# Sixty product slabs in each feed-forward part, eight short last tiles

## The chip, the cores and the metric

The kernel runs on one core of one Trainium2 chip. Times are device microseconds of one execution. A row of the trace names an engine: PE does matrix products (PEld its weight loads), DVE elementwise work, ACT scalar functions and copies, POOL a few DMAs, and SP issues most of the weight transfers. A matrix product sums into a bank, 128 partitions by 512 fp32 columns of the accumulator memory; DVE and ACT read banks from there.

## What is computed

A decoder trunk of two layers on 256 tokens of width 2048, in fp32. What the change touches is the feed-forward step at the end of both layers, a squared-ReLU map to width 8192 and back:

```python
D_MODEL = 2048
D_FF = 4 * D_MODEL
...
def squared_relu_mlp(h, w1, w2):
    z = jax.nn.relu(h @ w1)
    return (z * z) @ w2
...
for i in range(DEPTH):
    if i == N_A_LAYERS:
        sk1, sk2, sv = shared_kv(x, kv_norm, w_kv, k_norm, cos, sin)
    ...
    x = x + jnp.concatenate([token_out, mem_out], axis=-1) @ w_out[i]
    x = x + squared_relu_mlp(rms_norm(x, ffn_norm[i]), w_ff1[i], w_ff2[i])
return x
```

## The kernel before, in words

**Two halves of a number.** PE's fast fp32 format keeps only part of an fp32 number. Every operand is therefore held as a rounded half `hi` and a remainder `lo`, and a product is hi x hi + lo x hi + hi x lo. Weights arrive as fp32 from DRAM (`Feed.load`), in blocks of 128x128 grouped by four. A quad is prepared by a cast on ACT (L177) and a subtraction on DVE (L178) into the rings `hi_ring` and `lo_ring`, six slots of 512 columns. The feed makes these preparations in one fixed list and runs three of them ahead of the job that PE is at (`AHEAD` in `fill`). Both engines work off their queues in order, so a late split holds whatever stands behind it.

**Ordinary tiles.** `a_part` multiplies a block by the 256 tokens in two matmuls: L430 has `hi` as the fixed operand and streams the tokens' [hi | lo] side by side, 512 columns, and L432 has `lo` and streams 256 columns. The two halves of the bank must then be added on DVE after an eviction by ACT (L758). `c_tile` makes the same product as three matmuls of 256 columns (L444 to L446), all into one half of a bank, so nothing has to be added afterwards.

**A feed-forward part** (`ffn`, called for l = 0 and l = 1) takes the stretches from about 252 to 928 us and from about 1325 us to the end. It computes 64 up tiles of 128 units each (`up_tile`): 16 blocks of `w_ff1`, eviction L758, add L815, ReLU (L819 to L823), square L826 into `stage`, and from there `convert` splits the result into `z` and forms, for every pair of tiles, four sums of quarter blocks (`combine`, L790 to L793; `sums_low`). Later, and partly in between, it multiplies by `w_ff2`.

**Slabs.** Most of the product with `w_ff2` is done by a Strassen-Winograd scheme: two blocks of rows by two times 512 columns are multiplied by seven products instead of eight. Such a piece is a slab (`slab_jobs`): four jobs with 1 or 2 products each, a product being three 512-column matmuls (L861, L863, L864), summed in seven banks. The weights of a slab need sums as well: `first_sum` brings the sum of two transfers by a DMA on SP's queue and an accumulating one on POOL's (L152), and `_prepare` makes two further ones on DVE (L201, L215). There are two column groups: g = 1 holds output tiles 0 to 7, g = 0 tiles 8 to 15, and both use the same seven banks. When the group changes, `swap` copies the seven banks to SBUF (L928) and the other group's back (L920, in `restore`), all on ACT. Rows are grouped in batches of four slabs, h; the order of the groups is 0 1, 1 0, 0 1 and so on, so the group changes once a batch. A slab of index i needs the up tiles 2i and 2i+1 with their sums. There are 56 slabs in a part (`PER_PART`): i = 0 to 23 in both groups, then i = 24 to 31 in group 0 alone. Then five swaps take place and, at the last change, `close_left`, which folds the seven banks of group 1 with DVE and ACT into four quarters. `turn_left` transposes these on PE (L973) and adds them to the residual.

**When the slabs run.** `early` and `late` give the up tile at which each slab is due. `due` issues the jobs that are due, every four blocks of an up tile; it stops when 16 jobs (four slabs) are left. `at(d, ...)` puts a follow-up operation d ticks later; a tick comes with every job and every quad.

**The end of a part** is `last`. What group 1 has not done with slabs, the rows of up tiles 48 to 63, is done as eight down tiles 0 to 7 of 16 blocks each (`down_tile`: `a_part`, eviction, add, multiply by the row scale, add to the residual). In the second part the last one, n = 7, uses `c_tile` and needs no eviction. The 16 left jobs stand between quads of these tiles (`ends`). `finish_banks`, at tile 5, folds group 0's banks, and its four transposed pieces (`ct`, L1012) follow some ticks later. As each output tile is complete, `done(n)` starts the next stage's preparation with it (first part: `x_kv`, L326) or its transfer to the output (second part).

A scheduler orders the program on each engine; `feed.order` adds an order between two instructions without a wait. One such order puts the ReLU of tile 2 behind the last cast issued before it (L821).

Of the kernel before, what the change touches and what calls it, by code (L numbers as in the profile page):

```python
# [18 lines left out]
T = 256  # L19
# [4 lines left out]
NH = 725  # L24
NBLK = 5796
SLOTS, AHEAD, LOADS, RAWS = 6, 3, 3, 4
PER_PART = 56
CN = 0.5 ** (1.0 / 3.0)
LNC = math.log(CN)

# [68 lines left out]
class Feed:  # L99


    def __init__(self, tc, wst, wpool, rows, plan, dry):
        self.tc, self.nc, self.wst, self.wpool, self.rows = tc, tc.nc, wst, wpool, rows
        self.plan, self.dry = plan, dry
        self.pos = 0
        self.slab_no = 0
        self.lp = self.pp = 0
        self.raw = {}
        self.split = {}
        self.t1 = None  # L110
        self.loads_ahead = LOADS
        self.t1_of = [None] * 3
        self.behind = None
        self.gate = None
        if not dry:
            self.hi = wpool.tile([P, SLOTS * 512], F32R, name="hi_ring")
            self.lo = wpool.tile([P, SLOTS * 512], F32R, name="lo_ring")
            self.busy = [False] * SLOTS
            self.at = 0
# [52 lines left out]
    def _split(self, job, src, n):  # L172
        a = self._slots(n)
        if a is None:
            return False
        hi, lo = self.hi[:, a * 512 : (a + n) * 512], self.lo[:, a * 512 : (a + n) * 512]
        self.last_cast = self.nc.scalar.copy(hi, src)  # L177
        low = self.nc.vector.tensor_sub(lo, src, hi.bitcast(F32))  # L178
        if job[0] == "S":
            self.last_low = low  # L180
        if self.behind:
            self.order(low, self.behind)
            self.behind = None
        self.split[job] = (hi, lo, range(a, a + n))
        return True
# [103 lines left out]
def program(ctx, tc, plan, dry, xT, memT, par, lam, cst, wst, yT):  # L289
# [437 lines left out]
    def ffn(l, xs, tags, done):  # L727
# [27 lines left out]
        def evict(ps):  # L755
            x = outs[cnt[0] % 2]
            cnt[0] += 1
            nc.scalar.copy(x, ps)  # L758
            return x

        def when(ready, fn):
            fn() if ready() else at(1, lambda: when(ready, fn))
# [45 lines left out]
        def up_tile(i, ps, between=None):  # L808
            a_part(ps, "w_ff1", l, i, range(NK), xs, between=between)
            if i == 0:  # L810
                r.append(rstd_from("x"))
                at(3, lambda: r.append(columns("x", "o")[1]))
                at(6, lambda: nc.scalar.activation(r[0], r[0], AF.Square))
            y = evict(ps)[:, 0 : 2 * T]
            at(1, lambda: nc.vector.tensor_add(y[:, 0:T], y[:, 0:T], y[:, T : 2 * T]))  # L815
            d = 3 if i == 2 else 2

            def relu():
                one = nc.scalar.activation(y[:, 0:T], y[:, 0:T], AF.Relu)  # L819
                if i == 2 and not dry:  # L820
                    feed.order(one, feed.last_cast.ins.name)  # L821

            at(d, relu)  # L823

            def square():
                nc.scalar.activation(stage[i % 8], y[:, 0:T], AF.Square)  # L826
                at(1, lambda: convert(i))

            at(d, square, 2)

        def down_tile(n, ps, between=None):
            ks = range(3 * NK, 4 * NK)
            if l == 1 and n == 7:
                c_tile(ps, "w_ff2", l, n, ks, z)
                x = outs[cnt[0] % 2]
                nc.vector.tensor_mul(x[:, 0:T], ps[:, 0:T], r[0])
                nc.vector.tensor_add(resid[:, n, :], resid[:, n, :], x[:, 0:T])
                done(n)
                return
            a_part(ps, "w_ff2", l, n, ks, z, between=between)  # L840
            x = evict(ps)

            def add():
                nc.vector.tensor_add(x[:, 0:T], x[:, 0:T], x[:, T : 2 * T])
                nc.vector.tensor_mul(x[:, 0:T], x[:, 0:T], r[0])
                nc.vector.tensor_add(resid[:, n, :], resid[:, n, :], x[:, 0:T])
                done(n)

            at(1, add)
# [116 lines left out]
        def turn_left(h):  # L966
            t4 = bank().rearrange("p (c t) -> p c t", c=2)
            sides = ((left["c11"], left["c12"]), (left["u"], left["v"]))
            for e in range(2):
                n = (2 * h + e) // 4  # L970
                w = (2 * h + e) % 4 * P
                for t in range(2):
                    nc.tensor.transpose(  # L973
                        t4[:, e, t * P : t * P + P], sides[t][n][:, w : w + P], ident
                    )
            x = evict(t4.rearrange("p c t -> p (c t)"))
            c = 2 * h

            def add():
                two = x.rearrange("p (c t) -> p c t", c=2)  # L980
                nc.vector.tensor_add(resid[:, c : c + 2, :], resid[:, c : c + 2, :], two)

            at(1, add)
# [35 lines left out]


        slabs = []
        for h in range(6):
            for g in (0, 1) if h % 2 == 0 else (1, 0):
                slabs += [(g, 4 * h + i, g == h % 2) for i in range(4)]
        slabs += [(0, i, False) for i in range(24, 32)]
        jobs = [(s, j) for s in range(len(slabs)) for j in range(4)]
        runs = {}

        def one_job():
# [4 lines left out]
                runs[s] = slab_jobs(g, i, again, end)  # L1034
            runs[s](j)
            if end and s + 1 < len(slabs):
                if g == 1 and i == 23:
                    at(1, lambda: close_left(j))
                else:
                    at(3 if j == 3 else 2, lambda: swap(j, 1 - g))  # L1040

        early = (4, 6, 8, 10, 11.5, 12.5, 13.5, 14.5, 15, 16, 17.5, 19, 20.5)
        late = (58, 59.5, 61, 62.5, 64)

        def tiles_at(s):

            if s < 13:
                return early[s]
            if s >= 48:
                return late[s - 48]  # L1050
            return early[12] + (s - 12) * (late[0] - early[12]) / 36

        def due(tiles, least=0):
            n = 0
            while len(jobs) > 16:
                s, j = jobs[0]
                if tiles_at(s) + j * (tiles_at(s + 1) - tiles_at(s)) / 4 > tiles and n >= least:
                    break
# [8 lines left out]
        for i in range(4, 64):  # L1067
# [3 lines left out]
                due(i, 1)  # L1071
            up_tile(i, bank(), lambda b, i=i: due(i + b / 16) if b > 0 and b % 4 == 0 else None)
        due(64)
        assert len(jobs) == 16 and not turns
        feed.loads_ahead = LOADS

        ends = (
            (1, 1, 1, 0), (1, 1, 1, 0), (1, 1, 1, 1), (1, 0, 1, 0), (1, 0, 1, 0), (2, 0, 0, 0),
        )

        def last():
            def some(n):
                for _ in range(n):
                    one_job()
                    tick()

            def between(n):
                return lambda b: some(ends[n][b // 4]) if b > 0 and b % 4 == 0 else None

            for n in range(8):  # L1090
                if n < 6:
                    some(ends[n][0])
                if n == 5:
                    finish_banks()
                ps = bank() if n < 6 else mmt("ff2")
                down_tile(n, ps, between(n) if n < 6 else None)

        return last

# [549 lines left out]
```

## Time and profile before

| | us |
|---|---|
| median of 3 runs (2007.15 to 2007.61) | 2007.27 |
| the profiled execution, whole | 2007.09 |
| its span, first to last instruction | 2005.3 |
| DVE busy in the span | 1757.0 |
| ACT busy in the span | 1500.0 |

By stretches of the profiled execution, busy microseconds:

| stretch | length | PE | DVE | ACT | POOL |
|---|---|---|---|---|---|
| first feed-forward part, 252 to 928 | 676.00 | 674.84 | 622.04 | 534.57 | 50.16 |
| second feed-forward part, 1325 to 2002 | 677.00 | 675.02 | 616.47 | 525.36 | 50.04 |

The transfers move 420.09 MB, 209 GB/s on average. In a timeline row stand the start, the duration, the engine, the line, the operation, what it writes and from what, and its shape; an entry in brackets is the time that the engine stood idle before it, and what ended that. PE overlaps successive matmuls, so the busy time of PE hides short delays and the distance from start to start shows them.

### The profile page before, as it was taken

What the parts mean: (1) busy time and instruction counts of PE and PEld (TensorE: products, weight loads), DVE (VectorE), ACT (ScalarE), POOL (GpSimd) and SP (SyncE); (2) the same over time, 40 slices, a digit from 0 to 9 for tenths busy, and PEclk for the clock granted to TensorE, in tenths of its full rate; (3) what the DMA queues carried; (4) which work ended last, traced back from release to release, by engine and by line L of the source; (5) the groups of instructions that cost most, each with busy time, mean ns of one, the idle gap of its engine ahead of it and who ended that gap; (6) DMA issues with size and microseconds to landing.
All of it is one profiled execution on the core that took longest, in us unless ns stands there. A gap on an engine that the chain in (4) does not pass through costs nothing.

```text
span 2005.3 us, 31837 instructions
## 1 busy us (share of the span) xinstructions
PE 1997.1 (100%) x10534; PEld 1702.4 (85%) x10534; DVE 1757.0 (88%) x3089; ACT 1500.0 (75%) x2791; POOL 149.9 (7%) x179
## 2 busy tenths in 40 slices
PE   9999999999999999999999999999999999999999
PEld 8888888888888888888888888888888888888888
DVE  8888878989989899999765698878989899999997
ACT  7765577787887878778665699567787878888775
POOL 0001310000000000000000000320000000000000
PEclk9999999999999999999999999999999999999999
DMA  9556577777777777755576534567777777777774
GB/s 319 172 189 192 188 211 217 230 219 234 226 227 226 227 232 209 226 182 187 183 233 196 168 127 137 196 198 221 224 222 231 220 235 225 227 231 214 221 221 134
DMA packets 142725, 420.09 MB, mean 209 GB/s; under 512 B 16096, under 2 KB 18784, under 8 KB 142560
## 3 DMA queue, kind: packets, MB, share of 16 engines
q1 hardware_dynamic: 126288, 388.69, 58.6%
q0 software_dynamic: 16128, 29.37, 9.1%
q8 instruction: 82, 1.34, 0.3%
q14 instruction: 83, 0.68, 0.1%
q10 hardware_dynamic: 144, 0.01, 0.0%
HBM read 415.90 MB, written 2.10 MB: 208 GB/s over the span
## 4 chain that ended last, share of the span: by engine, by line
PE 96%; DVE 1%; ACT 1%; DMA 0%; issue 0%; SPq 0%; ACTq 0%; DVEq 0%
PE x_bank L430 24%; PE x_bank L432 12%; PE p L861 9%; PE p L864 9%; PE p L863 9%; PE wo L430 6%; PE wo L432 3%; PE u L430 2%; PE ff L430 1%; PE u L432 1%; PE q L464 1%; PE k L464 1%; PE q L466 1%; PE q L465 1%; PE k L466 1%; PE v L464 1%
## 5 line engine op out<-in xcount | busy, mean ns | idle before, releaser
L177 ACT CAST hi_ring<-raw 128x512 fp32r<-128x512 f32 x1001 | 609.9, 621 | 265.8 <-PE x_bank L430 61.5
L178 DVE TENSOR_TENSOR lo_ring<-raw,hi_ring 128x512 fp32r<-128x512 f32 x1001 | 680.0, 694 | 108.9 <-ACT hi_ring L177 96.6
L430 PE MATMUL x_bank<-fx,hi_ring 128*128 128x512 f32 x1952 | 611.0, 394 | 1.0 <-ACT room L758 1.0
L432 PEld LDWEIGHTS x_bank<-fx,lo_ring 128*128 128x128 f32 x1952 | 366.3, 188 | 85.2 <-DVE lo_ring L178 2.1
L178 DVE TENSOR_TENSOR lo_ring<-slab,hi_ring 128x1024 fp32r<-128x1024 f32 x280 | 342.0, 1221 | 58.4 <-ACT hi_ring L177 56.5
L177 ACT CAST hi_ring<-slab 128x1024 fp32r<-128x1024 f32 x280 | 294.2, 1052 | 120.7 <-PE x_bank L430 64.6
L432 PE MATMUL x_bank<-fx,lo_ring 128*128 128x256 f32 x1952 | 384.4, 278 | 0.0
L430 PEld LDWEIGHTS x_bank<-fx,hi_ring 128*128 128x128 f32 x1952 | 318.2, 189 | 24.8 <-ACT room L758 2.9
L152 POOL DMA_DIRECT2D room<-in_w x112 | 96.8, 868 | 1129.4 <-DMA room<-in_w 1109.5
L861 PE MATMUL p<-hi_ring,sit 128*128 128x512 f32 x448 | 177.2, 395 | 0.6 <-ACT hi_ring L177 0.5
L863 PE MATMUL p<-hi_ring,sit 128*128 128x512 f32 x448 | 175.5, 392 | 0.0
L864 PE MATMUL p<-lo_ring,sit 128*128 128x512 f32 x448 | 174.8, 391 | 0.5 <-DVE lo_ring L178 0.5
L430 PE MATMUL wo<-cat,hi_ring 128*128 128x512 f32 x512 | 161.9, 397 | 0.3 <-DVE rc L401 0.3
L178 DVE TENSOR_TENSOR lo_ring<-room,hi_ring 128x512 fp32r<-128x512 f32 x168 | 144.8, 863 | 6.9 <-ACT hi_ring L177 6.9
L177 ACT CAST hi_ring<-room 128x512 fp32r<-128x512 f32 x168 | 128.5, 765 | 23.7 <-PE x_bank L430 17.1
L861 PE MATMUL p<-hi_ring,z 128*128 128x512 f32 x336 | 131.5, 391 | 0.0
L864 PE MATMUL p<-lo_ring,z 128*128 128x512 f32 x336 | 130.9, 390 | 0.5 <-DVE lo_ring L178 0.5
L863 PE MATMUL p<-hi_ring,z 128*128 128x512 f32 x336 | 131.2, 391 | 0.0
L432 PEld LDWEIGHTS wo<-cat,lo_ring 128*128 128x128 f32 x512 | 96.0, 188 | 21.9
L864 PEld LDWEIGHTS p<-lo_ring,sit 128*128 128x128 f32 x448 | 84.2, 188 | 21.2 <-DVE lo_ring L178 3.2
L432 PE MATMUL wo<-cat,lo_ring 128*128 128x256 f32 x512 | 101.6, 279 | 0.0
L861 PEld LDWEIGHTS p<-hi_ring,sit 128*128 128x128 f32 x448 | 84.0, 187 | 11.8 <-ACT hi_ring L177 3.2
(374 smaller groups left out, 3348.8 us busy)
## 6 DMA issues: line engine op xcount, KB each, us to landing
raw<-in_w SPq DMA_DIRECT2D x500, 512.0 KB, 4.3
slab<-in_w SPq DMA_DIRECT2D x112, 512.0 KB, 4.3
room<-in_w SPq DMA_DIRECT2D x168, 256.0 KB, 3.4
room<-in_w POOLq DMA_DIRECT2D x112, 256.0 KB, 5.8
slab<-in_w SPq DMA_DIRECT2D x56, 256.0 KB, 4.5
memraw<-in_mem SPq DMA_DIRECT2D x5, 512.0 KB, 4.5
resid<-in_x SPq DMA_DIRECT2D x8, 256.0 KB, 5.2
out_y<-resid SPq DMA_DIRECT2D x16, 128.0 KB, 1.9
```

Of the source, the lines that this page charges most:

```text
L152: self.nc.gpsimd.dma_start(self.t1[i], right, accum_op=ALU.add)
L177: self.last_cast = self.nc.scalar.copy(hi, src)
L178: low = self.nc.vector.tensor_sub(lo, src, hi.bitcast(F32))
L430: nc.tensor.matmul(ps, hi, xs[:, k, :], start=first and c == 0, stop=False)
L432: nc.tensor.matmul(ps[:, T : 2 * T], lo, xs[:, k, 0:T], start=False, stop=last and c == len(ks) - 1,)
L464: nc.tensor.matmul(ps[t], x[t][1], hi, start=k == 0, stop=False)
L465: nc.tensor.matmul(ps[t], x[t][0], hi, start=False, stop=False)
L466: nc.tensor.matmul(ps[t], x[t][0], lo, start=False, stop=k == NK - 1)
L861: nc.tensor.matmul(ps, a[1], hi, start=new, stop=False, **again)
L863: nc.tensor.matmul(ps, a[0], hi, start=False, stop=False, **again)
L864: nc.tensor.matmul(ps, a[0], lo, start=False, stop=end, **again)
```

## The change

- A part has 60 slabs in place of 56: group 1 gets i = 24 to 27 as well, and group 0 runs i = 28 to 31 last. The batches are now seven, in the group order 0 1, 1 0, 0 1, 1 0, 0 1, 1 0, 1 0, and then 0. The group changes eight times: seven swaps and the closing of group 1.
- The eight down tiles take the rows of up tiles 56 to 63, 8 blocks in place of 16. In both parts the tiles n = 3 to 7 are made by `c_tile`, as three 256-column products a block, in a bank of the tag `mm` and without an eviction.
- Eight jobs (two slabs) are left for `last` in place of 16: four ahead of tile 0, two ahead of tile 1, two ahead of tile 2. They stand ahead of the tiles, not between their quads. `finish_banks` comes at tile 2.
- The slabs' due tiles are spread evenly from tile 20 to tile 64; the first twelve have their own list, the last four are no longer denser.
- `evict` also returns the instruction. The three casts that are issued next after tile 3's eviction are ordered behind it (`cast_behind`), and the ReLU and the square of tile 2 come five ticks after their tile, not three.

```diff
-PER_PART = 56
+PER_PART = 60
...
         self.last_cast = self.nc.scalar.copy(hi, src)
+        if self.cast_behind:
+            self.order(self.last_cast, self.cast_behind.pop())
...
-            nc.scalar.copy(x, ps)
-            return x
+            return x, nc.scalar.copy(x, ps)
...
-            y = evict(ps)[:, 0 : 2 * T]
+            y, out = evict(ps)
+            if i == 3 and not dry:
+                feed.cast_behind = [out.ins.name] * 3
             at(1, lambda: nc.vector.tensor_add(y[:, 0:T], y[:, 0:T], y[:, T : 2 * T]))
-            d = 3 if i == 2 else 2
+            d = 5 if i == 2 else 2
...
         def down_tile(n, ps, between=None):
-            ks = range(3 * NK, 4 * NK)
-            if l == 1 and n == 7:
+            ks = range(56, 64)
+            assert all(k in z_done for k in ks)
+            if n >= 3:
                 c_tile(ps, "w_ff2", l, n, ks, z)
...
         slabs = []
-        for h in range(6):
-            for g in (0, 1) if h % 2 == 0 else (1, 0):
-                slabs += [(g, 4 * h + i, g == h % 2) for i in range(4)]
-        slabs += [(0, i, False) for i in range(24, 32)]
+        for h, first in enumerate((0, 1, 0, 1, 0, 1, 1)):
+            for g in (first, 1 - first):
+                slabs += [(g, 4 * h + i, g == first) for i in range(4)]
+        slabs += [(0, i, False) for i in range(28, 32)]
...
-                if g == 1 and i == 23:
+                if g == 1 and i == 27:
                     at(1, lambda: close_left(j))
...
-        early = (4, 6, 8, 10, 11.5, 12.5, 13.5, 14.5, 15, 16, 17.5, 19, 20.5)
-        late = (58, 59.5, 61, 62.5, 64)
+        early = (4, 6, 8, 10, 11.4, 12.4, 13.4, 14.4, 15.4, 16.4, 17.4, 18.8)
         def tiles_at(s):
-            if s < 13:
-                return early[s]
-            if s >= 48:
-                return late[s - 48]
-            return early[12] + (s - 12) * (late[0] - early[12]) / 36
+            return early[s] if s < 12 else 20 + (s - 12) * 44 / 46
         def due(tiles, least=0):
             n = 0
-            while len(jobs) > 16:
+            while len(jobs) > 8:
...
-        ends = (
-            (1, 1, 1, 0), (1, 1, 1, 0), (1, 1, 1, 1), (1, 0, 1, 0), (1, 0, 1, 0), (2, 0, 0, 0),
-        )
         def last():
-            def some(n):
-                for _ in range(n):
+            for n in range(8):
+                for _ in range((4, 2, 2, 0, 0, 0, 0, 0)[n]):
                     one_job()
                     tick()
-            def between(n):
-                return lambda b: some(ends[n][b // 4]) if b > 0 and b % 4 == 0 else None
-            for n in range(8):
-                if n < 6:
-                    some(ends[n][0])
-                if n == 5:
+                if n == 2:
                     finish_banks()
-                ps = bank() if n < 6 else mmt("ff2")
-                down_tile(n, ps, between(n) if n < 6 else None)
+                down_tile(n, bank() if n < 3 else mmt("ff2"))
```

More of the change, by code (lines that the diff above doesn't have):

```diff
@@ L113, in __init__ @@
         self.behind = None
+        self.cast_behind = []
         self.gate = None
@@ L825, in square @@
             def square():
+                assert i < 8 or i - 8 in z_done
                 nc.scalar.activation(stage[i % 8], y[:, 0:T], AF.Square)
@@ L840, in down_tile @@
             a_part(ps, "w_ff2", l, n, ks, z, between=between)
-            x = evict(ps)
+            x, _ = evict(ps)
             def add():
@@ L975, in turn_left @@
                     )
-            x = evict(t4.rearrange("p c t -> p (c t)"))
+            x, _ = evict(t4.rearrange("p c t -> p (c t)"))
             c = 2 * h
@@ L1073, in ffn @@
         due(64)
-        assert len(jobs) == 16 and not turns
+        assert len(jobs) == 8 and not turns
         feed.loads_ahead = LOADS
-        ends = (
-            (1, 1, 1, 0), (1, 1, 1, 0), (1, 1, 1, 1), (1, 0, 1, 0), (1, 0, 1, 0), (2, 0, 0, 0),
-        )
         def last():
-            def some(n):
-                for _ in range(n):
+            for n in range(8):
+                for _ in range((4, 2, 2, 0, 0, 0, 0, 0)[n]):
                     one_job()
                     tick()
-            def between(n):
-                return lambda b: some(ends[n][b // 4]) if b > 0 and b % 4 == 0 else None
-            for n in range(8):
-                if n < 6:
-                    some(ends[n][0])
-                if n == 5:
+                if n == 2:
                     finish_banks()
-                ps = bank() if n < 6 else mmt("ff2")
-                down_tile(n, ps, between(n) if n < 6 else None)
+                down_tile(n, bank() if n < 3 else mmt("ff2"))
         return last
```

## The prediction

> **What bounds the kernel now.** I read the page first (busy time, granted clock, chain of waits), then busy time by stretches of the two feed-forward parts, then timelines of the stretches where something is not full.
>
> ```profile
> PE 1997.1 (100%) x10534; PEld 1702.4 (85%) x10534; DVE 1757.0 (88%) x3089; ACT 1500.0 (75%) x2791; POOL 149.9 (7%) x179
> PE 96%; DVE 1%; ACT 1%; DMA 0%; issue 0%; SPq 0%; ACTq 0%; DVEq 0%
> ```
>
> PE fills the span and is 96% of the chain that ends last, so removed PE time is worth its full length as long as nobody makes PE wait. The next engine is DVE. By stretches (columns: length, then busy time of PE, PEld, DVE, ACT, POOL, granted clock, DMA share, GB/s):
>
> ```profile
> 450.00:550.00 100.00, 100.00 (x515) 84.77 (x514) 92.53 (x141) 80.17 (x136) 8.63 (x10) 1.00 0.75 226
> 764.00:784.00 20.00, 19.69 (x98) 15.85 (x97) 19.94 (x29) 17.52 (x30) 1.72 (x2) 1.00 0.65 194
> 784.00:824.00 40.00, 40.00 (x211) 33.44 (x211) 39.72 (x66) 31.42 (x52) 2.59 (x3) 1.00 0.77 229
> 864.00:904.00 40.00, 40.00 (x211) 34.06 (x210) 36.80 (x59) 27.76 (x48) 0.86 (x1) 1.00 0.51 166
> ```
>
> The clock is full (1.00) in every stretch. In the middle of a part DVE has 7.5% to spare and PE never waits. From the closing of the left column group (764) to 824 DVE is 99.4% busy (59.66 of 60), and that is where PE loses a little; by 864 DVE has 8% to spare again. This stretch decides how much of the change's gain is kept.
>
> **The PE work.** PE matmuls overlap, so one costs the distance between starts, not its duration:
>
> ```profile
> 1980.08 0.40 PE L861 MATMUL p<-hi_ring,sit 128*128 128x512 f32 x1
> ...
> 1982.81 0.62 PE L430 MATMUL x_bank<-z,hi_ring 128*128 128x512 f32 x2
> ...
> 1988.37 0.63 PE L430 MATMUL ff<-z,hi_ring 128*128 128x512 f32 x2
> ...
> 1998.49 0.36 PE L444 MATMUL ff<-z,hi_ring 128*128 128x256 f32 x1
> 1998.69 0.28 PE L445 MATMUL ff<-z,hi_ring 128*128 128x256 f32 x1
> ...
> 2001.32 0.28 PE L446 MATMUL ff<-z,lo_ring 128*128 128x256 f32 x1
> ```
>
> Twelve slab products stand between the first two rows: 2.73/12 = 0.2275 us each, so a slab of 21 takes 4.78. A full down tile of 16 blocks (512 + 256 columns each) lies between the second and third: 5.56, 0.3475 a block. Between the last two are 22 starts of the 256-column form: 0.1195 each, 0.3585 a block. In each part four slabs are added (19.11) and eight half tiles removed (8 x 2.78 = 22.24); five remaining half tiles change from 2.78 to 24 x 0.1195 = 2.87 (0.45). Part one: -2.68. In part two the last tile has the 256-column form already: 19.11 - 7 x 2.78 - 2.87 + 4 x 0.09 = -2.86. Together -5.54; I take -5.2, because a change of form costs up to 0.08 at its first matmul (0.20 to the next start after the row of 1998.49, against 0.12 later) and the built order has more changes of form near the end. Ends: -5.5 and -4.6.
>
> The Trainium skill (TensorE: Matmul & The Clock Gate, Back-to-back issue gap) gives an isolated warm gap of N/2.4 + 2.5 ns, 109 ns for 256 columns and 216 ns for 512, by which the 256-column form would cost nothing extra (327 against 325 ns a block, an estimate); the 131 ns that it gives for sustained 512-column products are not seen here (0.2275). Its Perfetto Trace Analysis page (Matmuls) says that larger matmuls are the more efficient. The rows side with that: 0.011 us on each of 64 more such blocks, 0.7 in all; by the gap rule the sum below would be 0.7 lower.
>
> **The start of the slabs.** PE waits here now:
>
> ```profile
> 274.80 0.39 PE L863 MATMUL p<-hi_ring,z 128*128 128x512 f32 x1
> 275.72 0.50 PE L864 MATMUL p<-lo_ring,z 128*128 128x512 f32 x1 [0.53 <-DVE lo_ring L178]
> 276.98 0.40 PE L863 MATMUL p<-hi_ring,sit 128*128 128x512 f32 x1
> 277.65 0.50 PE L864 MATMUL p<-lo_ring,sit 128*128 128x512 f32 x1 [0.28 <-DVE lo_ring L178]
> ...
> 1349.72 0.49 PE L864 MATMUL p<-lo_ring,sit 128*128 128x512 f32 x1 [0.27 <-DVE lo_ring L178]
> 1351.22 0.73 PE L430 MATMUL x_bank<-fx,hi_ring 128*128 128x512 f32 x2 [1.01 <-ACT room L758]
> ...
> 1349.55 1.13 ACT L177 CAST hi_ring<-raw 128x512 fp32r<-128x512 f32 x2
> 1350.59 0.57 ACT L758 COPY room<-x_bank 128x512 f32<-128x512 f32 x1
> ```
>
> Against 0.23 the starts are 0.69, 0.44 and, in part two, 1.27 late; the last because tile 3's eviction (L758) stands behind casts on ACT. The new ordering puts the next three casts behind that eviction. In the built order it moves ahead of tile 4's casts in both parts: what is queued behind it on ACT is only those casts, whose readers come a slab job (0.7) and more later. In part one, one cast (0.5) leaves the queue ahead of slab 0's, and the second slab split moves ahead of the wide subtraction (L215) on DVE. I count 0.5 + 0.4 in part one and 1.2 in part two: -2.1. Ends: 0 (the wait only moves to the split) and -2.4. The later relu of tile 2 (5 ticks for 3) is not needed until slab 1, two tiles on: nothing.
>
> **Two more swaps a part.** Grouping seven row batches instead of six makes seven swaps and the closing out of five and the closing; each copies seven banks out and back on ACT:
>
> ```profile
> 508.20 0.40 PE L863 MATMUL p<-hi_ring,sit 128*128 128x512 f32 x1
> 508.52 0.51 PE L864 MATMUL p<-lo_ring,sit 128*128 128x512 f32 x1
> 508.87 0.40 PE L861 MATMUL p<-hi_ring,z 128*128 128x512 f32 x1
> 585.00:610.00 25.00, 25.00 (x131) 21.13 (x130) 21.91 (x33) 23.87 (x44) 1.72 (x2) 1.00 0.74 227
> ```
>
> Late here are 0.09 + 0.12 of the swap that runs at 508 (0.32 and 0.35 between the starts, for 0.23). The last row is the whole of another, at 585 to 610: its 14 copies fill ACT to 95% (23.87 of 25), and PE is full beside it. So 0.2 each at most where I looked, and four more of them: +0.8. Ends: 0 and what the second rival below gives.
>
> **DVE at the end of a part.** DVE costs, again by starts:
>
> ```profile
> 775.44 1.22 DVE L178 TENSOR_TENSOR lo_ring<-slab,hi_ring 128x1024 fp32r<-128x1024 f32 x1
> 776.58 0.68 DVE L178 TENSOR_TENSOR lo_ring<-room,hi_ring 128x512 fp32r<-128x512 f32 x1
> 777.18 1.22 DVE L215 TENSOR_TENSOR slab<-room,slab 128x1024 f32<-128x1024 f32 x1
> 778.32 0.42 DVE L774 TENSOR_TENSOR z<-stage,z 128x256 fp32r<-128x256 f32 x1
> 778.66 1.29 DVE L178 TENSOR_TENSOR lo_ring<-raw,hi_ring 128x512 fp32r<-128x512 f32 x2
> ...
> 926.99 2.07 DVE L326 SCALAR_TENSOR_TENSOR x_kv<-resid,param,x_kv 128x256 fp32r<-128x256 f32 x5
> 928.97 1.29 DVE L178 TENSOR_TENSOR lo_ring<-raw,hi_ring 128x512 fp32r<-128x512 f32 x2
> 768.66 0.39 PE L863 MATMUL p<-hi_ring,sit 128*128 128x512 f32 x1
> 769.28 0.50 PE L861 MATMUL p<-hi_ring,sit 128*128 128x512 f32 x1 [0.23 <-ACT hi_ring L177]
> ```
>
> That is 1.14 for 1024 columns, 0.60 for 512, 0.34 for 256, and 0.40 for L326; the sums of 128 columns (L790 to L793) lie between nothing and 0.34, and I take 0.25, nearer to the 256-column row. A slab costs DVE 4 x 1.14 + 2 x 0.60 = 5.8 and PE 4.8; an up tile costs DVE 3.9 (four splits, L815, L774, half a set of sums) and PE 5.6. So every slab in place of blocks moves work towards DVE. In the middle the slabs go from 36 in 37.5 tiles to 46 in 44: DVE's share from (3.9 + 0.96 x 5.8)/(5.56 + 0.96 x 4.78) = 93% to 94%, still covered. At the end it is not. I counted both built orders from the first split of the left group's last slab to the third weight quad of the next stage (part one) or the end (part two). Before: DVE 36 of 1024, 99 of 512, 40 of 256, 15 L326, 24 of 128 = 126 against 132 of PE in part one, 118 against 129 in part two. After: 35, 89, 32, 14, 16 = 113.7 against PE's 187 slab products, 128 blocks, 120 short products, 32 transposes and 14 wide ones = 108.1 (transposes at a 256-column start, less a little: 0.11; the 14 are the next stage's); in part two 106.9 against 104.7. DVE goes from 6 below PE to 5.6 above in part one, and 2.2 above in part two. It carries in at most the three preparations that the feed runs ahead, 3 x 1.3 = 3.9; I take 3.2, as its idle share in the middle says that it is mostly at that limit. At 99.4% busy it adds 0.6. Part one: 5.6 + 0.6 - 3.2 = 3.0, of which 0.4 to 0.6 is paid now (the 0.62 between the last two rows, where 0.23 is due, and smaller ones): +2.4. Part two: nothing. Ends: 0 (in the quoted run to 928.97 DVE spends 2 us on one group before a split and PE does not wait) and 5.6.
>
> Hidden: the four slabs' two more DMAs each (one on SP's queue, one on POOL's, where POOL is 7% busy) and 0.26 MB a slab against a DMA share of 0.75. The last slab's sums are now made during the eight jobs after tile 63, two jobs before they are read: late by at most one split, inside the 3.0. The end of the program keeps its shape (half a tile after the last transposes, then a store).
>
> **Sum.** -5.2 - 2.1 + 0.8 + 2.4 = -4.1. The profiled execution took 2007.09 (span 2005.3); the median of the runs is 0.18 above it. So 2003.0 for a profiled one, 2003.2 for a median.
>
> **Rivals.**
> *All covered*: DVE's lead takes the whole of its excess, as it took the burst before 928.97. Then -5.2 - 2.1 + 0.4 = -6.9 + 0.18: 2000.4. For it: PE ran through 784 to 824 at 100% (40.00) with DVE at 99%. Against: it has no slack to rebuild a lead until the part ends.
> *Swaps bind*: ACT, already at 95% of a swap's stretch, gets 0.08 slab a tile more to cast, and all 14 swaps, not only four, cost 0.4 each instead of 0.2: 14 x 0.4 - 10 x 0.2 = 3.6 in place of 0.8, so 2006.0. For it: ACT's row. Against: DVE's split, not the cast, is what the late PE rows name.
> *Slower*: DVE is the bound from the closing of the left group to the end of each part but at less than a full share, because casts, evictions and banks stop it in turn. At 95%: 113.7/0.95 - 108.1 = 11.6 and 106.9/0.95 - 104.7 = 7.8; less twice the lead 13.0, against the 6.5 of the first three terms: 2013.8. It passes the time before when DVE's share falls below some 98%. For it: 36.80 of 40 is what DVE reaches where PE leads. Against: 59.66 of 60 where DVE leads.
>
> **Chances.** Forecast 0.40 (own range 2001.8 to 2005), all covered 0.30, swaps bind 0.18, slower 0.12. A measurement of this kernel tells 0.2% (4.0 us) from no change, so faster is below 2003.26: all of the second case and just over half of the first, 0.52; within 0.2%: the rest of the first and the third, 0.36; slower 0.12. The range for 8 in 10 runs from 1999.4 (all covered, with the far ends of PE work and start) to 2009 (into the slower case).
>
> **What would show it.** Fewer PE idles at the first two slabs and no eviction wait before tile 4 (start); PE's total starts down by 5; DVE at 99% from the closing to the first quads of the next stage, with PE waiting for L178's successor there in part one and not at the end of part two (DVE term); late starts of 0.2 at seven swaps a part. Wrong if DVE idles in that stretch while PE waits, or if PE waits at the middle of a part.

## The result and the profile after

The changed kernel took 2011.12 us (median of 12 runs, 2009.87 to 2012.92), the kernel before 2007.37 (12 runs): ratio 1.0019, interval 1.0011 to 1.0027. It is slower by about 3.7 us, where 2003.2 was forecast and the range ended at 2009. The profiled execution has a span of 2010.7 us, 5.35 more than that of before (2010.66 against 2005.32 from the trace). This execution took 2012.43 us, 1.3 above the kernel's median, so the table below explains 5.35 us of which the medians show 3.75.

The page of the changed kernel, busy time and chain by engine:

```profile
PE 1999.0 (99%) x10510; PEld 1696.5 (84%) x10510; DVE 1779.2 (88%) x3096; ACT 1525.3 (76%) x2838; POOL 157.1 (8%) x187
PE 93%; ACT 3%; DVE 2%; issue 1%; DMA 0%; ACTq 0%; DVEq 0%
```

PE's share of the chain falls from 96% to 93%, ACT's rises from 1% to 3% and DVE's from 1% to 2%.

To place the loss I added up what each distance between two starts on PE exceeds the distance of an undisturbed stream (0.2277 us for 512 columns, 0.1193 for 256, 0.109 for 128). This sum is called late starts below. The rest is PE's own work, and work plus late starts is the time from PE's first start to its last. In us:

| | before | after |
|---|---|---|
| PE's work | 1969.8 | 1964.4 |
| late: start of the slabs, part one / two | 2.5 / 2.5 | 1.6 / 0.9 |
| late: middle of the part, with its swaps | 1.2 / 1.2 | 3.2 / 3.4 |
| late: from the closing of group 1 on, some 66 us | 1.7 / 1.75 | 2.4 / 2.4 |
| late: end of the part, and the next stage's first quads | 0.25 / 0.2 | 6.5 / 1.15 |
| last start on PE to the end of the span | 4.0 | 4.4 |

PE's work falls by 5.46 as the slabs and half tiles say. Late starts rise by 10.4, and 0.4 comes at the tail: -5.46 + 10.44 + 0.37 = +5.35. The largest items are the end of part one (+6.2) and the middles with their swaps (+4.2); the closings bring 1.4 and the end of part two 1.0, and the starts save 2.5. The row of the starts and that of the middles vary between profiles, as shown below.

**The end of part one.** Busy time by stretches of the changed kernel (columns as in the prediction's table):

```profile
832.00:852.00 20.00, 19.34 (x96) 15.10 (x95) 19.89 (x30) 17.76 (x31) 1.73 (x2) 1.00 0.78 217
852.00:872.00 20.00, 19.95 (x104) 16.45 (x104) 19.30 (x31) 14.94 (x25) 1.73 (x2) 1.00 0.83 243
872.00:892.00 20.00, 20.00 (x108) 16.51 (x107) 18.66 (x30) 14.56 (x24) 0.86 (x1) 1.00 0.56 172
892.00:902.00 10.00, 10.00 (x48) 7.96 (x47) 10.00 (x15) 7.75 (x14) 0.00 (x0) 1.00 0.34 107
...
926.00:930.00 4.00, 3.44 (x26) 3.00 (x25) 4.00 (x11) 2.43 (x7) 0.00 (x0) 1.00 0.14 56
930.00:934.00 4.00, 2.10 (x8) 1.07 (x7) 3.66 (x10) 3.41 (x8) 0.00 (x0) 1.00 0.37 131
934.00:938.00 4.00, 4.00 (x11) 3.13 (x12) 3.16 (x7) 1.58 (x4) 0.00 (x0) 0.57 0.48 146
938.00:942.00 4.00, 4.00 (x19) 3.31 (x18) 3.78 (x8) 3.99 (x11) 0.00 (x0) 1.00 0.49 163
```

DVE is full at the closing, then has 0.70 and 1.34 us to spare up to 892 while PE is full, and from 892 it is full again until PE stands still for nearly half of 930 to 934. So there are two bursts, not one long one. Between them DVE's spare time is lost. I put that down to the feed, which keeps no more than three preparations in hand; the run with four, below, bears this out only in part. At 934 to 938 the clock (0.57) is down as well. What PE waits for and what DVE does meanwhile, in the timelines of the two engines:

```profile
927.57 0.40 PE L468 MATMUL k<-hi_ring,x_kv 128*128 128x512 f32 x1
928.53 0.38 PE L449 MATMUL ff<-z,lo_ring 128*128 128x256 f32 x1 [0.56 <-DVE lo_ring L181]
...
930.29 0.39 PE L468 MATMUL k<-hi_ring,x_kv 128*128 128x512 f32 x1
931.88 0.50 PE L467 MATMUL k<-hi_ring,x_kv 128*128 128x512 f32 x1 [1.20 <-DVE room L842]
...
932.92 0.39 PE L468 MATMUL k<-hi_ring,x_kv 128*128 128x512 f32 x1
934.00 0.94 PE L469 MATMUL k<-lo_ring,x_kv 128*128 128x512 f32 x2 [0.70 <-DVE lo_ring L181]
...
935.17 0.63 PE L468 MATMUL k<-hi_ring,x_kv 128*128 128x512 f32 x1
935.60 0.63 PE L469 MATMUL k<-lo_ring,x_kv 128*128 128x512 f32 x1
```

```profile
926.67 0.87 DVE L329 SCALAR_TENSOR_TENSOR x_kv<-resid,param,x_kv 128x256 fp32r<-128x256 f32 x2
927.46 0.42 DVE L843 TENSOR_TENSOR resid<-resid,room 128x256 f32<-128x256 f32 x1
927.79 1.29 DVE L181 TENSOR_TENSOR lo_ring<-raw,hi_ring 128x512 fp32r<-128x512 f32 x2
928.99 0.48 DVE L329 SCALAR_TENSOR_TENSOR x_kv<-resid,param,x_kv 128x256 fp32r<-128x256 f32 x1
929.39 1.28 DVE L1019 TENSOR_TENSOR resid<-resid,ct 128x512 f32<-128x512 f32 x2
931.01 0.49 DVE L329 SCALAR_TENSOR_TENSOR x_kv<-resid,param,x_kv 128x256 fp32r<-128x256 f32 x1 [0.34 <-ACT x_kv L411]
931.41 0.42 DVE L842 TENSOR_TENSOR room<-ff,r_x 128x256 f32<-128x256 f32 x1
931.74 1.27 DVE L329 SCALAR_TENSOR_TENSOR x_kv<-resid,param,x_kv 128x256 fp32r<-128x256 f32 x3
```

PE needs a split (L181), or the product with the row scale (L842) that frees a tile's bank. Both stand on DVE behind work whose result PE wants only later: remainders of x_kv (L329) and sums of the transposed pieces (L1019). The wait of 1.20 us names a bank of a 256-column tile, which the next stage's second row block wants. That gave two theories: DVE's burst, or the late release of these banks.

**A swap.** A swap's 14 copies, saves (L934) and restores (L926), stand on ACT between the casts (L178) that the next slab needs. ACT and PE at two swaps of part one, at 415 and at 496 us:

```profile
415.59 0.60 ACT L934 COPY keep<-p 128x512 f32<-128x512 f32 x1
416.07 0.60 ACT L934 COPY room<-p 128x512 f32<-128x512 f32 x1
416.55 1.14 ACT L926 COPY p<-room 128x512 f32<-128x512 f32 x2
417.59 0.44 ACT L831 ACTIVATE stage<-room 128x256 f32<-128x256 f32 x1
417.90 1.06 ACT L178 CAST hi_ring<-slab 128x1024 fp32r<-128x1024 f32 x1
...
501.62 0.62 ACT L934 COPY room<-p 128x512 f32<-128x512 f32 x1
502.10 0.45 ACT L831 ACTIVATE stage<-room 128x256 f32<-128x256 f32 x1
502.42 0.62 ACT L926 COPY p<-room 128x512 f32<-128x512 f32 x1
502.93 1.08 ACT L178 CAST hi_ring<-slab 128x1024 fp32r<-128x1024 f32 x1
```

```profile
418.55 0.39 PE L435 MATMUL x_bank<-fx,lo_ring 128*128 128x256 f32 x2
419.01 0.50 PE L867 MATMUL p<-hi_ring,sit 128*128 128x512 f32 x1
...
419.82 0.39 PE L869 MATMUL p<-hi_ring,z 128*128 128x512 f32 x1
420.27 0.50 PE L870 MATMUL p<-lo_ring,sit 128*128 128x512 f32 x1
...
503.51 0.39 PE L435 MATMUL x_bank<-fx,lo_ring 128*128 128x256 f32 x2
504.06 0.50 PE L867 MATMUL p<-hi_ring,z 128*128 128x512 f32 x1 [0.16 <-ACT hi_ring L178]
```

At both places the slab's product starts as its cast ends (417.90 + 1.06 and 502.93 + 1.08), and this cast stood behind copies. PE is late by 0.23 and 0.32. At 420.27 it is late by 0.22 again, as the split follows the cast.

What a swap costs depends on its place. Late starts around each swap that has restores (the first of a part has none), part one, in us:

| swap at | changed kernel | remainders put off | group 1 first | four saves on DVE |
|---|---|---|---|---|
| 415 | 0.96 | 0.29 | 0.27 | 0.20 |
| 496 | 0.52 | 0.51 | 0.52 | 0.11 |
| 578 | 0.32 | 0.33 | 0.31 | 0.05 |
| 659 | 0.18 | 0.18 | 0.18 | 0.14 |
| 740 | 0.52 | 0.50 | 0.50 | 0.12 |
| 780 | 0.33 | 0.34 | (none there) | 0.05 |

The last three columns are variants of the experiments below. Their swaps up to 740 are those of the changed kernel, in the last column with four copies moved to DVE. Part two repeats these numbers to within 0.03 except at its first full swap (one with restores), which cost 1.20 in the changed kernel's profile and 0.29, 1.03 and 0.19 in the others. So 1.6 of the 4.2 us by which the middles grew stand at these two swaps in this profile and not where the remainders were put off; what sets them there stays open. The middles of that run are 2.5 and 2.4 in place of 3.2 and 3.4: the changed kernel's swaps add between 2.5 and 4.2 us. In the kernel before, the four such swaps of part one cost 0.23, 0.43, 0.19 and 0.24.

### The profile page after: what moved, and what is told of

It is laid out like the page before. It is cut to its first block, busy times and chain, and to the rows that moved or that the text cites. A ratio compares the mean times of both kernels' runs of the same rounds, so it can differ in the third digit from the quotient of the medians.

```text
span 2010.7 us, 31966 instructions
## 1 busy us (share of the span) xinstructions
PE 1999.0 (99%) x10510; PEld 1696.5 (84%) x10510; DVE 1779.2 (88%) x3096; ACT 1525.3 (76%) x2838; POOL 157.1 (8%) x187
## 3 DMA queue, kind: packets, MB, share of 16 engines
q8 instruction: 82, 1.34, 0.3%
## 4 chain that ended last, share of the span: by engine, by line
PE 93%; ACT 3%; DVE 2%; issue 1%; DMA 0%; ACTq 0%; DVEq 0%
PE x_bank L433 21%; PE x_bank L435 11%; PE p L867 9%; PE p L870 9%; PE p L869 9%; PE wo L433 6%; PE wo L435 3%; PE u L433 2%; ACT hi_ring L178 1%; PE ff L433 1%; PE u L435 1%; PE k L469 1%; PE q L467 1%; PE q L469 1%; PE q L468 1%; PE v L468 1%
## 5 line engine op out<-in xcount | busy, mean ns | idle before, releaser
L178 ACT CAST hi_ring<-raw 128x512 fp32r<-128x512 f32 x969 | 593.5, 623 | 267.3 <-PE x_bank L433 61.1
L181 DVE TENSOR_TENSOR lo_ring<-raw,hi_ring 128x512 fp32r<-128x512 f32 x969 | 662.0, 695 | 105.1 <-ACT hi_ring L178 93.5
L181 DVE TENSOR_TENSOR lo_ring<-slab,hi_ring 128x1024 fp32r<-128x1024 f32 x300 | 366.4, 1221 | 50.1 <-ACT hi_ring L178 48.8
L178 ACT CAST hi_ring<-slab 128x1024 fp32r<-128x1024 f32 x300 | 314.6, 1053 | 117.2 <-PE p L869 65.0
L867 PE MATMUL p<-hi_ring,sit 128*128 128x512 f32 x480 | 190.5, 397 | 0.4 <-ACT hi_ring L178 0.2
L869 PE MATMUL p<-hi_ring,sit 128*128 128x512 f32 x480 | 187.9, 391 | 0.0
L870 PE MATMUL p<-lo_ring,sit 128*128 128x512 f32 x480 | 186.5, 391 | 0.2
L181 DVE TENSOR_TENSOR lo_ring<-room,hi_ring 128x512 fp32r<-128x512 f32 x180 | 154.3, 863 | 5.7 <-ACT hi_ring L178 5.6
L178 ACT CAST hi_ring<-room 128x512 fp32r<-128x512 f32 x180 | 138.1, 769 | 19.0 <-PE p L869 9.5
L867 PE MATMUL p<-hi_ring,z 128*128 128x512 f32 x360 | 141.2, 392 | 0.7 <-ACT hi_ring L178 0.7
L869 PE MATMUL p<-hi_ring,z 128*128 128x512 f32 x360 | 140.6, 391 | 0.0
L870 PE MATMUL p<-lo_ring,z 128*128 128x512 f32 x360 | 139.7, 392 | 0.0
```

The source lines that it names most:

```text
L867: nc.tensor.matmul(ps, a[1], hi, start=new, stop=False, **again)
L869: nc.tensor.matmul(ps, a[0], hi, start=False, stop=False, **again)
L870: nc.tensor.matmul(ps, a[0], lo, start=False, stop=end, **again)
```

## The experiments

Times are medians of runs taken beside runs of the kernel before, and ratios are against those. Two variants are compared by what each is above the kernel before in its own runs; for the changed kernel that is 3.75 us. Late starts are from one profile each. Those at a part's first slabs differ between profiles (0.8 to 2.4 in part one for kernels with the same order there), so differences of a microsecond aren't read out of that row.

**The start orderings alone.** The kernel before with the hunks of `cast_behind` and the later ReLU (all in the diff above).

> The kernel before with the start orderings alone (three casts behind tile 3's eviction, the ReLU of tile 2 at five ticks). Theory: these alone give the 0.9 us that the first part and the 1.7 us that the second part gain at their first slabs, so 2007.4 - 2.7 = 2004.7. Rival: the gain there comes from the other due times of the first slabs, and this is 2007.4 as before.

2005.66 us (before 2007.06), ratio 0.9992, 0.9983 to 1.0001. Late starts at the first slabs fall from 2.5 and 2.5 to 1.8 and 1.35, so 1.8 of the 2.5 that the changed kernel gains there comes from these orderings; the median shows 1.4, in an interval that just reaches no change. The rest can't be told from the spread of this place.

**One group change fewer.**

```diff
-        for h, first in enumerate((0, 1, 0, 1, 0, 1, 1)):
+        for h, first in enumerate((1, 0, 1, 0, 1, 0, 1)):
...
-        holds = [0] * 7
+        holds = [1] * 7
```

> The changed kernel with group 1 first, so that the groups change seven times a part (six swaps and the closing) in place of eight. Theory that swaps now bind (PE's late starts outside start, closing and end went from 2.5 us at ten swaps to 6.8 us at fourteen, 0.49 each): two fewer, 2011.1 - 1.0 = 2010.1, and each swap left still costs about 0.5. Rival: the late starts come from the denser slabs, wherever the group changes, and are kept: 2011.1.

2009.45 us, ratio 1.0013 (1.0004 to 1.0023), 2.4 above the kernel before and so 1.4 below the changed one. Late starts in the middle go from 3.2 and 3.4 to 2.1 and 2.9, and the end of part one keeps its 6.4. By the table of swaps, the one that is left out in each part had cost 0.33, so two bring 0.7. The rest of the fall stands at the first full swap, whose cost varies; the other swaps keep theirs. A swap less thus saves what it cost at its place.

**The adds of the short tiles on POOL.**

```diff
-                nc.vector.tensor_add(resid[:, n, :], resid[:, n, :], x[:, 0:T])
+                eng = nc.vector if l == 1 and n == 7 else nc.gpsimd
+                eng.tensor_add(resid[:, n, :], resid[:, n, :], x[:, 0:T])
```

> The changed kernel with the residual add of the 256-column down tiles on POOL in place of DVE (five in the first part, four in the second). Theory that DVE's work at the end of a part is the bound: 5 x 0.34 us less on DVE in the first part, 4 x 0.34 in the second, so 1.7 us less there and up to 1.0 in the second: 2008.4 to 2009.4. Theory that the late release of the banks of these tiles is the bound: the add comes after the release, the wait of 1.2 us at the next stage's second bank stays, and the time is 2010.5 to 2011.1 (slower, if POOL is late with the residual).

2012.44 us, ratio 1.0027 (1.0016 to 1.0038): no gain. POOL's timeline in this run, and DVE's:

```profile
918.28 1.38 POOL L844 TENSOR_TENSOR resid<-resid,room 128x256 f32<-128x256 f32 x1 [42.31 <-DVE room L842]
922.13 1.72 POOL L844 TENSOR_TENSOR resid<-resid,room 128x256 f32<-128x256 f32 x1 [2.47 <-DVE room L842]
```

```profile
920.24 0.48 DVE L329 SCALAR_TENSOR_TENSOR x_kv<-resid,param,x_kv 128x256 fp32r<-128x256 f32 x1 [1.18 <-ACT x_kv L411]
...
924.43 0.48 DVE L329 SCALAR_TENSOR_TENSOR x_kv<-resid,param,x_kv 128x256 fp32r<-128x256 f32 x1 [1.18 <-ACT x_kv L411]
```

These two adds take 1.4 and 1.7 us (all nine 0.7 to 2.0) against 0.34 on DVE, and DVE then stands still twice for 1.18 us: L329 of the tile waits for the cast L411 that waits for POOL, and the splits stand behind it. The experiment does not tell the two theories apart, but shows that the place of L329 in DVE's queue matters, not its sum alone.

**The last tiles in the old form.**

```diff
-            if n >= 3:
+            if l == 1 and n == 7:
...
-                down_tile(n, bank() if n < 3 else mmt("ff2"))
+                down_tile(n, bank() if n < 6 else mmt("ff2"))
```

> The changed kernel with the last tiles in the 512 + 256-column form and an eviction on ACT, as before (all but the last tile of the second part). Theory of the banks: ACT frees them, the next stage's second bank has no wait (1.2 us less, perhaps the slow clock behind it too, 1.5), and PE has 0.8 less to do: 2007.6 to 2009.1. Theory of DVE's work: nine adds of 0.34 us more on DVE at the ends, 1.7 in the first part and 1.4 in the second, against 0.8 less on PE: 2012 to 2014.

2015.0 us, ratio 1.0036 (1.0024 to 1.0049). With the banks freed by ACT, PE's work 0.8 lower and nine adds more on DVE, it is 7.9 above the kernel before, 4.2 slower than the changed one. PE's late starts at the end of part one are 6.1, hardly fewer. The theory of the banks falls; the wait of 1.20 us was the face of a late DVE. The 256-column form, which costs PE 0.8 us, pays for itself by the adds that it saves.

**The remainders of x_kv one a quad.** Each L329 is put off to three quads ahead of its use:

```diff
+    def kv_done(n):
+        dst, g = x_in[0][:, n, :], gcol(G_KV + n)
+        nc.scalar.activation(dst[:, 0:T], resid[:, n, :], AF.Copy, scale=g)
+        left = 2 if n >= 12 else 4 if n >= 8 else (7 - n) * 2 - (n < 3)
+        at(left + n - 3, lambda: stt(
+            dst[:, T : 2 * T], resid[:, n, :], g, dst[:, 0:T].bitcast(F32), ALU.mult, ALU.subtract
+        ))
...
-    down = ffn(0, fx, ("S1", "S0"), lambda n: resid_done(n, [(x_in[0], G_KV)], False))
+    down = ffn(0, fx, ("S1", "S0"), kv_done)
```

> The changed kernel with the sixteen remainders of x_kv (L329, 0.40 us each on DVE) made one a quad in the next stage, three quads ahead of their use, in place of at once. Theory that DVE's burst at the end of the first part is the bound (6.5 us of late starts on PE from the last slabs to the first quads of the next stage): 5 to 6 us of L329 leave the burst, of which the next stage's spare time takes most; late starts there 2 to 3 in place of 6.5, the time 2007.1 to 2008.6. Rival that the wait is on the banks of the last tiles or on the feed's transfers: late starts as before, 2011.1.

2007.41 us, ratio 1.0 (0.9991 to 1.0009): 0.3 above the kernel before, 3.4 less than the changed one. Late starts at the end of part one fall from 6.5 to 1.1. Its stretches:

```profile
912.00:922.00 10.00, 10.00 (x86) 10.00 (x86) 10.00 (x21) 8.56 (x19) 0.00 (x0) 1.00 0.49 158
922.00:932.00 10.00, 10.00 (x71) 9.35 (x70) 10.00 (x22) 9.13 (x21) 0.00 (x0) 1.00 0.61 199
932.00:942.00 10.00, 10.00 (x45) 8.26 (x44) 10.00 (x25) 9.72 (x25) 0.00 (x0) 1.00 0.48 162
```

DVE does not become idle, it is full to 942. But PE is full beside it and the clock stays at 1.00: the same work in another order. That was the cause of 5.3 of the 6.2 us, the slow clock included. The medians differ by less, 3.4. The two rows that vary between profiles, 2.1 more here at the first slabs of both parts and 1.6 less at the first full swaps, do not explain that; it stays open.

**Four preparations ahead.**

```diff
-SLOTS, AHEAD, LOADS, RAWS = 6, 3, 3, 4
+SLOTS, AHEAD, LOADS, RAWS = 6, 4, 3, 4
```

> The changed kernel with the feed running four preparations ahead, not three. Theory that DVE idles before its bursts only because its lead is capped (2 us idle in the 40 us before 892): one preparation of 0.6 to 1.3 us more in hand at the end of each part and at each swap, so -1 to -3: 2008.1 to 2010.1. Rival that the ring of six slots, not the count, caps the lead: 2011.1.

2011.47 us, ratio 1.0022 (1.0013 to 1.0031): no gain. Late starts from the closing on fall by 0.6 in each part, those at the end of part one rise to 7.7. DVE's idle time between 852 and 892 falls from 2.0 to 1.4 only. A longer lead alone does not carry DVE through the second burst; whether the six slots or the order of the queue takes it away was not separated.

**Two of these together.** The order that begins with group 1, the remainders one a quad, and the squares (L717) thinner:

```diff
-        at(2 + n // 2, lambda n=n: later_square(n))
+        at(2 + 3 * n // 4, lambda n=n: later_square(n))
```

> The changed kernel with group 1 first (seven group changes a part), the remainders of x_kv one a quad, and the squares of the residual (L717) three in four quads, not two a quad. If the effects add: 2011.1 - 1.7 (group 1 first, as measured) - 2.5 to 4.0 (burst) = 2005.4 to 2006.9. If the burst only moves into the next stage: 2009.4.

2006.63 us, ratio 0.9996 (0.9988 to 1.0005): 0.5 below the kernel before, 4.2 below the changed one. The effects nearly add: 1.4 and 3.4 would make 4.8.

**Four of the fourteen copies of a swap on DVE.** In the changed kernel, in `swap`:

```diff
-                nc.scalar.copy(x, banks[p])
+                (nc.vector.tensor_copy if j >= 2 else nc.scalar.copy)(x, banks[p])
```

> The changed kernel with four of the fourteen copies of a swap (the saves of the last four banks) on DVE in place of ACT. Theory that ACT holds the casts of the first slab behind a swap back while DVE idles beside it: late starts in the middle of the parts, 3.2 and 3.4 us now, fall to 1.2 to 2.2 each: 2011.1 - 2 to 4 = 2007 to 2009. Rival that the slabs' density and DVE set them: DVE has 2.4 us more a swap, late starts stay or rise: 2011 to 2013.

2007.92 us, ratio 1.0007 (0.9998 to 1.0016): 1.3 above the kernel before, 2.5 below the changed one. Late starts in the middle fall from 3.2 and 3.4 to 0.8 and 0.8. Even against the 2.5 and 2.4 of the run with the remainders put off, this is 3.3 less, and each full swap became cheaper. With DVE having more to do, PE waits less; so ACT's queue at the swaps was the cause, not the density of the slabs on DVE.

**The three together.**

> The kernel with group 1 first, the remainders of x_kv one a quad and three squares in four quads, and four saves of a swap on DVE. Theory of ACT at the swaps: late starts in the middle fall from 2.1 to some 1 us in each part: 2006.6 - 1 to 2 = 2004.6 to 2005.6, faster than the kernel before by 1.5 to 2.5. Rival: 2006.6 or more.

2002.74 us, ratio 0.9977 (0.9967 to 0.9987). This beats both kernels: 3.9 us less than the kernel before. Its page, and its saves in the table of groups:

```profile
PE 1992.5 (100%) x10510; PEld 1695.7 (85%) x10510; DVE 1803.8 (90%) x3144; ACT 1489.1 (74%) x2762; POOL 156.7 (8%) x187
PE 97%; DVE 2%; issue 1%; ACT 0%; DMA 0%; SPq 0%; DVEq 0%
L934 DVE COPY room<-p 128x512 f32<-128x512 f32 x40 | 26.7, 684 | 2.8 <-PE p L870 2.8
```

ACT is gone from the chain. Late starts are 0.7 and 0.7 in the middle and 1.1 at both ends; 2.3 are left at either closing.

**Twice the group changes in the kernel before.**

```diff
-            for g in (0, 1) if h % 2 == 0 else (1, 0):
-                slabs += [(g, 4 * h + i, g == h % 2) for i in range(4)]
+            for g in (0, 1):
+                slabs += [(g, 4 * h + i, g == 0) for i in range(4)]
```

> The kernel before with the groups in the order 0 1 in every batch: twelve group changes a part in place of six, all else kept. If a swap costs what it does before the change (2.4 us of late starts at ten swaps, 0.24 each): 12 x 0.24 = 2.9, 2010.0. If what it does after (6.5 at fourteen, 0.47 each): 5.6, 2012.7. If the swaps cost nothing and the density of the slabs sets the late starts: 2007.1.

2019.88 us, ratio 1.0064 (1.005 to 1.0078): 13.2 more for twelve swaps, 1.1 each, above both expectations. By late starts 8.7 of it lie in the middle (5.5 and 5.6 in place of 1.2 and 1.2: 0.50 a swap at 22 swaps) and 4.5 from the closing on (4.0 and 4.0 in place of 1.7), where a swap now comes four slabs before. So the price of a swap is no constant: by place it runs from 0.2 to 1.1 here, and each place costs the same in both parts to within 0.03. What sets it beside the length of ACT's queue (how the copies fall against a tile's eviction and casts) was not separated.

**What 60 slabs are worth.** The start orderings and the four saves on DVE in the kernel before, with 56 slabs:

> The kernel before (56 slabs, 16-block last tiles) with the start orderings and four saves of a swap on DVE, to see what the slabs and short tiles are worth once the new waits are gone. Late starts: 2.5 us less at the starts at most (1.4 measured alone) and 0.5 less in the middle of each part: 2006.7 - 1.4 - 1.0 = 2004.3. The kernel of 60 slabs with the same saves was 2002.7; theory (5.25 us less PE work, given back at the closings, the ends and the two swaps left over): this one stays 1 to 3 us behind it. If the 60 slabs bring nothing, it is 2002.7 too.

2004.95 us, ratio 0.999 (0.998 to 0.9999). It is 2.3 below the kernel before, where the 60 slabs with the same saves are 3.9 below: some 1.7 for the slabs and short tiles, of the 5.46 that they take from PE (3.0 between the two profiled executions). The intervals of the two runs overlap, so the size is not settled. Nor are the slabs and tiles all that differs: the kernel of 60 slabs also has group 1 first, the remainders put off and thinner squares. At the end of part one, where the remainders act, the kernel before has only 0.25 us of late starts to lose. The saves brought little here (late starts in the middle 1.05 and 0.9 for 1.2): there was little to remove.

**The last tiles in the old form, in the fastest kernel.**

> The fastest kernel so far (60 slabs, group 1 first, the remainders of x_kv one a quad, saves on DVE) with its last tiles in the 512 + 256-column form and an eviction on ACT. PE has 0.8 us less to do, DVE nine adds of 0.34 more (3.1), at ends where it is still full. Theory that DVE is the bound there: 2003 to 2005.5, slower than 2002.7. If the burst is gone with the remainders of x_kv, PE's saving shows: 2001.9.

2005.87 us, ratio 0.9995 (0.9986 to 1.0003), 2.6 slower than with 256-column tiles (1.35 below the kernel before, not 3.9). Late starts at the ends go from 1.1 and 1.1 to 3.0 and 2.9, though the remainders of x_kv are out of the way. DVE is still the bound at the ends.

## Why the prediction was wrong

**PE's work: right.** -5.2 was taken; the trace shows -5.46, and the changes of form that I deducted appear among the late starts.

**Start: right in kind; its size can't be told.** -2.1 was taken, -2.5 measured in this profile. Over the profiles of kernels with 60 slabs the gain at the two starts runs from 0.4 to 3.0, and the start orderings alone showed 1.4 in the median. In part two the eviction no longer stands behind the casts. The rows of the changed kernel that answer to the wait of 1.27 us:

```profile
1354.87 0.39 PE L870 MATMUL p<-lo_ring,sit 128*128 128x512 f32 x1
1355.09 0.63 PE L433 MATMUL x_bank<-fx,hi_ring 128*128 128x512 f32 x2
1355.61 0.50 PE L435 MATMUL x_bank<-fx,lo_ring 128*128 128x256 f32 x2
```

**Swaps: wrong, +0.8 taken, +4.2 measured (+2.5 in another profile).** The step that failed is "0.2 each at most where I looked", given to the four that are added. It was read too low, for the swap at 508 cost 0.43 when all its late starts are counted, not the two that I quoted. And a swap has no one price: with the change the places moved, and ten of the twelve swaps with restores cost 0.18 to 0.52 each, the other two 0.96 and 1.20 in this profile. The rival of the swaps had the mechanism and nearly the price, 0.4 each against 0.35 to 0.47 as the mean of fourteen. I set it aside because the late rows named DVE's split, not the cast. But a split follows its cast, so a row that names the split says nothing against ACT, and at 504.06 the changed kernel's row names the cast itself. The four saves moved to DVE showed it.

**DVE in part one: wrong, +2.4 taken, +6.9 measured (0.7 at the closing, 6.2 at the end).** The place and the engine were right. The step that failed is the count "from the first split of the left group's last slab" with one lead of 3.2. DVE stood idle for 2 us of that stretch between its two bursts, while PE was full. What it does from 892 on had to be counted by itself; how much of the late starts these 2 us would have saved, no run separates. The second error is that I counted sums only: sixteen L329, the last of them wanted fifteen quads of the next stage later, stood ahead of splits wanted at once, and putting them off took away 5.3 us without any less work. A third item is the clock at that place (1.6 us), which I did not foresee. The group of five such remainders at 926.99 (L326 there) that I quoted as harmless had been so under the old load, and I carried it over to the new one in a rival.

**DVE in part two: wrong, nothing taken, +1.6 measured.** I had the lead of 3.2 cover an excess of 2.2; the closing brought 0.65 and the end 0.95. At both ends PE waits 0.25 at the first down tile for a split behind the last slabs' sums. The run with four preparations takes 0.6 off each closing, no run the rest of this.

**Not priced.** The tail (+0.37): I wrote that the end of the program keeps its shape. Its cause stays open.

**The slower rival** (2013.8) came nearest to the time, by a mechanism that holds only in part: DVE at less than a full share through the whole stretch. The runs show two bursts with a pause, and a quarter to two fifths of the added late starts at the swaps.

## What to carry to other kernels

An engine that is 90% busy and works in order has to be counted burst by burst, from its last idle moment, since its spare time in a pause did not carry over (2 us here). Look in its queue for work whose result is wanted late and which stands ahead of work wanted now: putting it off took away half of the late starts that this change had added. A price read at one place (a swap) holds only for that place, and a wait that names the last engine of a chain does not clear the engine ahead of it.

## What the hardware showed unexpectedly

PE's clock was halved for 3.41 us, from 934.36 to 937.77. The matmuls of 512 columns from 934.74 to 937.73 start 0.427 us apart, against 0.23, and the stretch 934 to 938 has a granted clock of 0.57. These starts cost some 1.6 us, a quarter of the loss at that place. The slow stretch followed idle times of 0.56, 1.20 and 0.70 us within some 6 us (the three waits quoted above). The same happened in the run with group 1 first, after the same waits, and in the run with four preparations ahead, after one of 2.5 us.

The Trainium skill (TensorE: Matmul & The Clock Gate, Why this matters for your kernels) puts the limit at idle gaps above some 3 us; here no gap was that long. The traces point to a sum. In all three runs the fall came a whole number of stretches of 3.413 us after the clock had first risen (272, 273 and 272 of them), and it lasted one. In the stretch just before the fall PE was idle for 1.64, 1.95 and 1.72 us, about half of it. In the run with four saves on DVE the same three waits came (0.58, 1.20 and 0.70 us), but lay across a border of two such stretches, with 1.26 and 0.80 us of idle time, and the clock stayed. It also stayed after 1.42 us in a later stretch of that run, and after 1.30 and 1.70 in two stretches of the run with POOL's adds. That fits a clock set by PE's idle sum in each stretch, with a limit near half. The limit isn't sharp here, as 1.70 without a fall stands beside 1.64 with one.

A residual add of 128x256 fp32 values took 0.7 to 2.0 us on POOL and 0.34 from start to start on DVE.
